# The first expert stage: 64 slots in fp32 for the seven experts with the fewest tokens, chosen on the chip

## The chip, the core and the metric

The kernel runs on one core of a Trainium2 chip. The metric is the device time of one launch in microseconds, the median of three runs. The engines in what follows are PE (TensorE, the matrix engine; PEld is its load of the stationary operand), DVE (VectorE), ACT (ScalarE), POOL (GpSimd) and SP (SyncE, which here issues the weight loads). Data comes from HBM over 16 DMA engines.

## What is computed

Two blocks in a row, on 256 tokens and 256 context tokens of width 1024. The first block has two layers; each ends in a routed mixture of 16 experts of which every token uses two. Layer 0 routes all 512 tokens, layer 1 only the 256 tokens. The second block has a third expert layer. The change is in layer 0's experts alone:

```python
def routed_moe(h2d, router_w, router_b, w_gate, w_up, w_down):
    ...                                   # every token: 2 experts of 16, weights wts
    counts = jnp.bincount(flat_e, length=N_EXPERTS)
    ...                                   # rows of the same expert brought together
    def expert_block(args):
        xblk, e = args
        hid = jax.nn.silu(xblk @ w_gate[e]) * (xblk @ w_up[e])
        return hid @ w_down[e]
```

Each weight matrix is 1024 by 1024 in fp32, 4 MiB, so an expert needs 12 MiB of weights. The 1024 assignments of a token to an expert are spread unevenly.

## The kernel before

The first expert stage is `moe0` (line 1172). `route_steps` ranks the experts for every token and gives each assignment a place among those of its expert; `counts` gives the number of assignments of each expert. From these a table `idx` of 16 columns is made: column x names the tokens of expert x, one in each of 128 slots. `gather(x)` (line 1219) brings these 128 rows from HBM by an indirect DMA on POOL's queue. `overflow` (line 1360) holds a loop for experts with more than 128 tokens. It stands in an `If` that every engine evaluates by loading one number from SBUF (lines 1370 and 1371); where no expert has more, all engines branch past it.

Then 16 experts follow, x = 0 to 15, in program order, each with three products: gate, up and down. They are staggered: up of x, gate of x + 1, down of x. A product (`product`, line 1556) has 8 steps `kt`. In each, the 128 by 1024 slice of the weight is split into `hi` (a copy to fp32r, on ACT, line 341) and `lo` (the rest, on DVE, line 329), and six matmuls of 512 columns add `xh·hi`, `xh·lo` and `xl·hi` for both column halves. The stationary operand is the tokens or the hidden values, transposed (`t8`, line 1540: eight transposes on PE, then `xh` on ACT and `xl` on DVE). Between the steps of a product stand, at step 2, `silu` and the product with `up`, and at step 5 the transposes that the next product needs. `store` writes the 128 rows of the expert to a DRAM tensor `yd`, from which at the end every token gathers its two rows.

Weights come through `wrows` (line 359): four tiles of 1 MiB for each matrix, from a ring of nine (`RING` is 7, and 2 more in this stage), issued by SP one after the other. SP waits for each ring place until the old tile is split. What stands in which order on an engine is decided by a scheduler when the program is built, by program order and the buffers that are free; each engine then works in that order. `u4`, a pool of 20 buffers of 128 by 1024, holds `hi`, `lo`, `xh`, `xl` and the rest; `u2` has three of 128 by 512.

The other two expert stages (`experts`, line 1717) already use column groups: with G = 2 in layer 1 there are 64 slots, and a step is two fp32 matmuls (line 1771), one for each column half of the unsplit weight, on columns 0 to 63 and 64 to 127 of PE.

Of the kernel before, what the change touches and what calls it, by code (L numbers as in the profile page):

```python
# [17 lines left out]
KT = 8  # L18
# [198 lines left out]
class K:  # L217
# [141 lines left out]
    def wrows(self, src, r0=0, n=1024, pairs=False):  # L359
# [8 lines left out]
        return Weights(tiles, 2)  # L368

# [740 lines left out]
    def route_steps(self, p, nb, l, after_counts=None):  # L1110
# [45 lines left out]
        e16 = self.C("e16").unsqueeze(1).to_broadcast([128, nb, 16])  # L1156
# [3 lines left out]
        def rest():  # L1160
            for k, oh in enumerate((oh1, oh2)):
                self.total(oh, e16, nb, out[:, k])
                self.total(oh, aff, nb, out[:, 4 + k])
# [6 lines left out]


    def moe0(self, X, htok, srow, kr, lg, modT):
# [42 lines left out]
        ti = self.sm(16)  # L1215
        self.copy(ti, pt[:, 0:16], "v")
        self.stt(idx, pt[:, 16:32], 128.0, ti, OP.mult, OP.add)

        def gather(x):
            xg = self.u4("xg")  # L1220
            nc.gpsimd.indirect_dma_start(
                out=xg, out_offset=None, in_=h2d[0:512],
                in_offset=bass.IndirectOffsetOnAxis(ap=idx[:, x:x + 1], axis=0))
            return xg

        xg = [gather(0), gather(1)]
        rest()
        ov = self.keep(8, "ov0").rearrange("p (k b) -> p k b", k=2)
        self.ts(ov, r, 127.5, op0=OP.is_gt)
        Wg, Wu, Wd = A["moe_w_gate"][0], A["moe_w_up"][0], A["moe_w_down"][0]  # L1230
        w = self.wrows(Wg[0], pairs=True)
# [8 lines left out]
        self.overflow(0, 512, 128, rt, cnt, ov, lambda: h2d, add)  # L1240


        last = 15 * 128
        pos = self.keep(8, "pos0").rearrange("p (k b) -> p k b", k=2)
        self.stt(pos, e, 128.0, r, OP.mult, OP.add)
# [13 lines left out]

        def silu(x, pg):  # L1260
            s[x] = self.u4("sg")
# [8 lines left out]
        def store(x, py):  # L1270
            y = self.u4("y") if x < 15 else held[2][:, 0]
            for half, p in enumerate(py):
                self.copy(y[:, half * 512:(half + 1) * 512], p, None if x == 15 else "s")
            if x < 15:
                nc.gpsimd.dma_start(yd[x * 128:(x + 1) * 128, :], y)
# [28 lines left out]
        for x in range(16):  # L1304
# [5 lines left out]
            def next_x(x=x):  # L1310
                if x < 15:
                    nxt["x"] = self.t8(xg[1])
# [3 lines left out]
            pu = self.product(xT, self.wrows(Wu[x], pairs=True) if x < 15 else wu, {2: flush, 5: next_x})  # L1316

            def hidden(x=x):
                nxt["h"] = self.t8(s.pop(x))

            if x < 15:
                xT = nxt["x"]
                pg = self.product(xT, self.wrows(Wg[x + 1], pairs=True), {2: lambda: times(x, pu), 5: hidden})
# [3 lines left out]
            if x < 15:  # L1327
                w = self.wrows(Wd[x], pairs=True)
            py = self.product(nxt["h"], w, {15: {2: collect}}.get(x, {}))
# [1364 lines left out]
```

## Time and profile before

| | |
|---|---|
| median of three runs | 2692.64 us (2692.07 to 2694.62) |
| profiled execution | 2689.91 us, of which the span from first to last instruction is 2688.1 us |
| busy in the span | PE 2324.9 us (86%), DVE 1401.4 us (52%), ACT 981.5 us (37%), POOL 61.3 us (2%) |
| HBM | 780.88 MB read, 295 GB/s over the span |
| first expert stage | about 485 to 1100 us |
| second expert stage | about 1329 to 1850 us |
| third expert stage | about 2230 to 2665 us |

Shares of the whole span mix stages with different limits. The rows below are taken from single stretches, whose limits in microseconds from the span's start each names. In a row of the view by stretch, "35.45 (x160)" is 35.45 us of busy time in 160 instructions. The DMA share is the mean busy share of the 16 DMA engines. A matmul in fp32 on a column group shows as two records.

### The profile page before, as it was taken

Reading aid. Unit: us, or ns where it says so; the run is one execution under the profiler, and the core shown is the slowest. Engines: PE = TensorE matmul, PEld = TensorE weight load, DVE = VectorE, ACT = ScalarE, POOL = GpSimd, SP = SyncE. Lnnn points to the kernel's source line nnn. Section 1 sums busy time; section 2 is a strip of 40 time slices with the busy share of each in tenths; the row PEclk is TensorE's granted clock in tenths of the full one; section 3 lists DMA queues with packets and bytes.
Section 4 is the critical chain, followed back from the end, with each engine's and each line's share of the span. In section 5 each row is a group of like instructions: output and inputs, shape, how many; then the busy total and the mean of one; then the engine's idle time right before and its main releaser. Section 6 shows DMA issues by size and latency. Waiting matters only on the chain.

```text
span 2688.1 us, 40516 instructions
## 1 busy us (share of the span) xinstructions
PE 2324.9 (86%) x16362; PEld 1589.2 (59%) x16363; DVE 1401.4 (52%) x2810; ACT 981.5 (37%) x1692; POOL 61.3 (2%) x57
## 2 busy tenths in 40 slices
PE   6999887799999999898898898997899977777765
PEld 4887666677777787675533443444888964323322
DVE  5675554888888888756314232324776751000001
ACT  3332332676767777446202221112545620000000
POOL 0000002000000001000000000000000000000000
PEclk8999999899999999999899999998899988777787
DMA  8157841799999998645499999987423449999997
GB/s 297 32 201 254 287 168 62 301 365 371 364 367 361 366 384 343 226 169 206 189 421 375 405 374 372 386 348 305 138 89 138 157 178 414 420 420 420 419 420 313
DMA packets 178600, 794.66 MB, mean 296 GB/s; under 512 B 18017, under 2 KB 33761, under 8 KB 104673
## 3 DMA queue, kind: packets, MB, share of 16 engines
q1 hardware_dynamic: 168048, 767.28, 73.3%
q0 software_dynamic: 5648, 20.45, 1.9%
q10 hardware_dynamic: 4704, 4.21, 0.5%
q8 instruction: 132, 2.16, 0.3%
q14 instruction: 68, 0.55, 0.1%
HBM read 780.88 MB, written 11.01 MB: 295 GB/s over the span
## 4 chain that ended last, share of the span: by engine, by line
PE 30%; DMA 20%; DVE 6%; ACT 1%; issue 1%; SPq 0%; DVEq 0%; ACTq 0%
PE ps L308 14%; PE ps L1771 7%; DMA w<-in_w_e_down_dram 6%; DMA w<-in_w_e_up_dram 5%; DMA w<-in_w_e_gate_dram 5%; PE ps L1785 4%; PE ps L1500 2%; PE ps L311 1%; DMA w<-in_moe_w_up_dram 1%; DMA w<-in_moe_w_down_dram 1%; DMA w<-in_w_in_dram 1%; PE ps L1713 1%; DVE sm L1664 1%; PE ps L1687 1%; DMA w<-in_moe_w_gate_dram 1%
## 5 line engine op out<-in xcount | busy, mean ns | idle before, releaser
L329 DVE TENSOR_TENSOR lo<-w,hi 128x1024 fp32r<-128x1024 f32 (+1 forms) x628 | 626.2, 1045 | 106.2 <-ACT hi L341 89.3
L341 ACT ACTIVATE hi<-w 128x1024 fp32r<-128x1024 f32 (+1 forms) x628 | 530.6, 913 | 95.6 <-PE ps L308 54.0
L1771 PE MATMUL ps<-w,xTs 128*32 128x256 f32 (+1 forms) x3072 | 405.9, 503 | 74.2 <-DMA w<-in_w_e_gate_dram 46.2
L1771 PEld LDWEIGHTS ps<-w,xTs 128*32 128x32 f32 (+1 forms) x3072 | 132.9, 128 | 291.2 <-issue 158.1
L1785 PE MATMUL ps<-w,hTs 128*32 128x256 f32 (+1 forms) x1536 | 217.2, 542 | 61.9 <-DMA w<-in_w_e_down_dram 53.6
L308 PE MATMUL ps<-lo,xh 128*128 128x512 f32 x768 | 243.0, 398 | 13.7 <-DVE lo L329 13.7
L308 PE MATMUL ps<-hi,xh 128*128 128x512 f32 x768 | 243.5, 398 | 7.5 <-ACT hi L341 7.5
L308 PE MATMUL ps<-hi,xl 128*128 128x512 f32 x768 | 238.0, 391 | 0.0
L1785 PEld LDWEIGHTS ps<-w,hTs 128*32 128x32 f32 (+1 forms) x1536 | 70.9, 136 | 191.0 <-issue 87.4
L308 PEld LDWEIGHTS ps<-lo,xh 128*128 128x128 f32 x768 | 141.1, 189 | 51.7 <-DVE lo L329 25.0
L308 PEld LDWEIGHTS ps<-hi,xh 128*128 128x128 f32 x768 | 140.6, 189 | 45.5 <-ACT hi L341 19.0
L308 PEld LDWEIGHTS ps<-hi,xl 128*128 128x128 f32 x768 | 144.6, 188 | 31.1
L329 DVE TENSOR_TENSOR sgs<-sgs,ps 128x512 f32<-128x512 f32 (+1 forms) x32 | 17.7, 553 | 266.2 <-PE ps L1771 266.2
L308 PE MATMUL ps<-hTh,hi 128*128 128x256 f32 x416 | 123.2, 296 | 0.8 <-ACT hi L341 0.8
L308 PE MATMUL ps<-hTh,lo 128*128 128x256 f32 x416 | 119.5, 287 | 2.0 <-DVE lo L329 2.0
L308 PE MATMUL ps<-hTl,hi 128*128 128x256 f32 x416 | 118.8, 286 | 0.0
L341 ACT ACTIVATE sgs<-ps 128x512 f32<-128x512 f32 (+1 forms) x32 | 15.7, 490 | 275.0 <-PE ps L1771 275.0
L308 PE MATMUL ps<-hh,hi 128*128 128x512 f32 (+1 forms) x272 | 106.1, 390 | 6.0 <-ACT hi L341 6.0
L308 PE MATMUL ps<-hl,hi 128*128 128x512 f32 (+1 forms) x272 | 101.1, 372 | 0.0
L308 PE MATMUL ps<-hh,lo 128*128 128x512 f32 (+1 forms) x272 | 101.0, 371 | 0.1
L320 ACT ACTIVATE hTs<-ps 128x512 f32<-128x512 f32 (+1 forms) x16 | 7.8, 490 | 234.9 <-PE ps L311 234.9
L341 ACT ACTIVATE xh<-ps 128x512 fp32r<-128x512 f32 x64 | 35.4, 595 | 135.8 <-PE ps L311 135.8
(567 smaller groups left out, 3650.7 us busy)
## 6 DMA issues: line engine op xcount, KB each, us to landing
w<-in_moe_w_gate_dram SPq DMA_DIRECT2D x128, 1024.0 KB, 7.7
w<-in_moe_w_up_dram SPq DMA_DIRECT2D x128, 1024.0 KB, 7.5
w<-in_moe_w_down_dram SPq DMA_DIRECT2D x128, 1024.0 KB, 9.0
w<-in_w_e_gate_dram SPq DMA_DIRECT2D x64, 1024.0 KB, 20.0
w<-in_w_e_down_dram SPq DMA_DIRECT2D x64, 1024.0 KB, 20.0
w<-in_w_e_up_dram SPq DMA_DIRECT2D x64, 1024.0 KB, 20.0
w<-in_ada_w_dram SPq DMA_DIRECT2D x48, 1024.0 KB, 7.1
w<-in_w_mod_dram SPq DMA_DIRECT2D x24, 1024.0 KB, 7.0
```

The source lines that it names most:

```text
L308: self.nc.tensor.matmul(out, lhsT, rhs, start=start, stop=stop)
L311: self.nc.tensor.transpose(out, in_, self.C("id"))
L320: self.nc.scalar.activation(out, in_, AF.Copy)
L329: self.nc.vector.tensor_tensor(out, a, b, op=op)
L341: self.nc.scalar.activation(out, in_, f, **kw)
L1500: self.nc.tensor.matmul(o, a[:, c].bitcast(FR), b, start=(k == 0 and j == 0 and m % 2 == 0), stop=(k == nk - 1 and j == 2), skip_group_che ...
L1664: nc.vector.tensor_reduce(mx, t, axis=AX.X, op=OP.max)
L1687: nc.tensor.matmul(po[j][0][r, c], v[n][:, g * 64:g * 64 + 64], at[i][:, n * 128:(n + 1) * 128], start=(n == 0), stop=(n == 3), tile_posit ...
L1713: self.nc.tensor.matmul(acc[b][dg], owT[r, b * 128:(b + 1) * 128], y[r, :n], start=(first and (b == 0 or G == 2)), stop=False, skip_group_ ...
L1771: self.nc.tensor.matmul(p[g * S:(g + 1) * S, :], a[:, s0:s0 + S], w(kt, g * n, (g + 1) * n), start=(kt == 0), stop=(kt == KT - 1), tile_po ...
L1785: self.nc.tensor.matmul(py[dg * S:(dg + 1) * S, :], hT[:, j * 128 + g * S:j * 128 + (g + 1) * S], w(ft, dg * n, (dg + 1) * n), start=(ft = ...
```

## The change

The experts are ranked on the chip by their number of assignments (`ranked`, DVE). Expert 0 is put first whatever its load, since its gate weights are loaded before the ranking is known. The next eight by load take the places 2, 4, ... 14 and 15, the seven smallest the places 1, 3, ... 13. A place of the first kind has 128 slots as before. One of the second kind, "few", has 64. Its tokens and hidden values are transposed but not split; its weights aren't split either; a step is two fp32 matmuls of 512 columns on 64 columns of PE each (`product` inside `moe0`). Its result lies with one column half on partitions 0 to 63 and the other on 64 to 127, and is stored by two DMAs. Which expert stands at a place is read by SP from SBUF into a register, and the weight loads take their address from it (`chosen`). The table `idx` is put into the new order, and positions and the test for the overflow loop go by the capacity of each expert.

```diff
+    def chosen(self, e, *W):
+
+        i = self.nc.values_load(e, engines=[mybir.EngineType.SP], min_val=0, max_val=15)
+        return [w[bass.ds(i, 1)].rearrange("a d f -> (a d) f") for w in W]
+
...
 
-        def rest():
+        def rest(more=()):
             for k, oh in enumerate((oh1, oh2)):
-                self.total(oh, e16, nb, out[:, k])
+                for row, o in more or ((self.C("e16"), out),):
+                    self.total(oh, row.unsqueeze(1).to_broadcast([128, nb, 16]), nb, o[:, k])
                 self.total(oh, aff, nb, out[:, 4 + k])
...
+    def ranked(self, cnt):
+        nc = self.nc
+        key, rank, place, base, cap, t = (self.sm(16) for _ in range(6))
+        e16 = self.C("e16")
+        self.stt(key, cnt, 16.0, e16, OP.mult, OP.add)
+        self.ts(key[:, 0:1], key[:, 0:1], 65536.0, op0=OP.add)
+        rows = lambda v: v.unsqueeze(1).to_broadcast([128, 16, 16])
+        cols = lambda v: v.unsqueeze(2).to_broadcast([128, 16, 16])
+        sel, w = (self.u2("place")[:, :256].rearrange("p (i e) -> p i e", i=16) for _ in range(2))
+        self.tt(w, rows(key), cols(key), OP.is_gt)
+        nc.vector.tensor_reduce(rank, w, axis=AX.X, op=OP.add)
+        self.ts(t, rank, 7.5, op0=OP.is_gt)
+        self.ts(place, rank, 8.0, 16.0, OP.is_equal, OP.mult)
+        self.stt(place, t, -17.0, place, OP.mult, OP.add)
+        self.stt(place, rank, 2.0, place, OP.mult, OP.add)
+        self.ts(base, place, 96.0)
+        self.stt(base, t, 32.0, base, OP.mult, OP.add)
+        self.ts(cap, rank, 8.5, -64.0, OP.is_gt, OP.mult)
+        self.ts(cap, cap, 128.0, op0=OP.add)
+        self.tt(sel, rows(place), cols(e16), OP.is_equal)
+        self.mul(w, sel, rows(e16))
+        expert = self.sm(16, I32, name="order")
+        self.reduce_int(expert, w)
+        return base, cap, sel, w, expert
+    def reduce_int(self, out, v):
+        t = self.sm(16)
+        self.nc.vector.tensor_reduce(t, v, axis=AX.X, op=OP.add)
+        self.copy(out, t, "v")
 
...
         idx = self.keep(16, "idx", I32)
-        ti = self.sm(16)
+        ti, tj, idx0 = self.sm(16), self.sm(16), self.sm(1, I32)
         self.copy(ti, pt[:, 0:16], "v")
-        self.stt(idx, pt[:, 16:32], 128.0, ti, OP.mult, OP.add)
+        self.stt(idx0, pt[:, 16:17], 128.0, ti[:, 0:1], OP.mult, OP.add)
+        self.stt(tj, pt[:, 16:32], 128.0, ti, OP.mult, OP.add)
+
+        few = lambda x: x % 2 == 1 and x < 15
+        slots = lambda x: slice(96 * x + 32 * (x % 2), 96 * x + 32 * (x % 2) + (64 if few(x) else 128))
 
         def gather(x):
-            xg = self.u4("xg")
+            xg, n = self.u4("xg"), 64 if few(x) else 128
+            at = (idx[:, x:x + 1] if x else idx0)[0:n]
             nc.gpsimd.indirect_dma_start(
-                out=xg, out_offset=None, in_=h2d[0:512],
-                in_offset=bass.IndirectOffsetOnAxis(ap=idx[:, x:x + 1], axis=0))
+                out=xg[0:n], out_offset=None, in_=h2d[0:512],
+                in_offset=bass.IndirectOffsetOnAxis(ap=at, axis=0))
             return xg
 
-        xg = [gather(0), gather(1)]
-        rest()
-        ov = self.keep(8, "ov0").rearrange("p (k b) -> p k b", k=2)
-        self.ts(ov, r, 127.5, op0=OP.is_gt)
-        Wg, Wu, Wd = A["moe_w_gate"][0], A["moe_w_up"][0], A["moe_w_down"][0]
-        w = self.wrows(Wg[0], pairs=True)
+        xg = [gather(0)]
+        base, cap, sel, tmp, order = self.ranked(cnt)
+        self.mul(tmp, sel, tj.unsqueeze(1).to_broadcast([128, 16, 16]))
+        self.reduce_int(idx, tmp)
+        xg.append(gather(1))
+        pos, capt = (self.keep(8, n).rearrange("p (k b) -> p k b", k=2) for n in ("pos0", "ov0"))
+        rest(((base, pos), (cap, capt)))
+
+        over = self.sm(8).rearrange("p (k b) -> p k b", k=2)
+        self.tt(over, r, capt, OP.subtract)
+        ov = capt
+        self.ts(ov, over, -0.5, op0=OP.is_gt)
+        self.tt(cap, cnt, cap, OP.subtract)
+        self.ts(cap, cap, 0.0, op0=OP.max)
+        self.add(pos, pos, r)
+        W = A["moe_w_gate"][0], A["moe_w_up"][0], A["moe_w_down"][0]
+        Wg, Wu, Wd = [u[0] for u in W]
+        w = self.wrows(Wg, pairs=True)
         ready = [self.wparts(w, kt) for kt in range(READY)]
 
...
-        self.overflow(0, 512, 128, rt, cnt, ov, lambda: h2d, add)
-        last = 15 * 128
-        pos = self.keep(8, "pos0").rearrange("p (k b) -> p k b", k=2)
-        self.stt(pos, e, 128.0, r, OP.mult, OP.add)
+        def all_tokens():
+            for k, oh in enumerate(self.oh):
+                self.total(oh, self.C("e16").unsqueeze(1).to_broadcast([128, 4, 16]), 4, e[:, k])
+            self.copy(r, over, "v")
+            return h2d
+        self.overflow(0, 512, 0, rt, cap, ov, all_tokens, add)
+        last = slots(15).start
         self.stt(pos, ov, 4096.0, pos, OP.mult, OP.add)
...
+        def product(x, a, w, inside={}):
+            if not few(x):
+                return self.product(a, w, inside)
+            p = self.ps()
+            for kt in range(KT):
+                if kt in inside:
+                    inside[kt]()
+                for g in range(2):
+                    nc.tensor.matmul(p[64 * g:64 * g + 64], a(kt), w(kt, 512 * g, 512 * g + 512), start=kt == 0,
+                                     stop=kt == KT - 1, tile_position=(0, 64 * g))
+            return [p]
+        def tokens_of(x, xg):
+            if not few(x):
+                return self.t8(xg)
+            p, t = self.ps(), self.u2("xf")
+            for k in range(KT):
+                nc.tensor.transpose(p[:, 64 * k:64 * k + 64], self.pair_block(xg[0:64], k), self.C("id")[0:64, 0:64])
+            self.copy(t, p)
+            return lambda kt: t[:, 64 * kt:64 * kt + 64]
+        def hidden_of(x, s):
+            if not few(x):
+                return self.t8(s)
+            p, t = self.ps(), self.u2("hf")
+            for j in range(4):
+                self.tr(p[:, 128 * j:128 * j + 128], self.pair_block(s, j))
+            self.copy(t, p)
+            return lambda ft: t[:, 128 * (ft % 4) + 64 * (ft // 4):128 * (ft % 4) + 64 * (ft // 4) + 64]
...
         def store(x, py):
+            if few(x):
+                y = self.u2("yf")
+                self.copy(y, py[0], "s")
+                for g in range(2):
+                    nc.gpsimd.dma_start(yd[slots(x)][:, 512 * g:512 * g + 512], y[64 * g:64 * g + 64])
+                return
...
             def next_x(x=x):
                 if x < 15:
-                    nxt["x"] = self.t8(xg[1])
+                    nxt["x"] = tokens_of(x + 1, xg[1])
                     if x < 14:
                         xg[1] = gather(x + 2)
 
-            pu = self.product(xT, self.wrows(Wu[x], pairs=True) if x < 15 else wu, {2: flush, 5: next_x})
+            pu = product(x, xT, self.wrows(Wu, pairs=True) if x < 15 else wu, {2: flush, 5: next_x})
 
             def hidden(x=x):
-                nxt["h"] = self.t8(s.pop(x))
+                nxt["h"] = hidden_of(x, s.pop(x))
 
             if x < 15:
                 xT = nxt["x"]
-                pg = self.product(xT, self.wrows(Wg[x + 1], pairs=True), {2: lambda: times(x, pu), 5: hidden})
+                down = Wd
+                Wg, Wu, Wd = self.chosen(order[0:1, x + 1:x + 2], *W)
+                pg = product(x + 1, xT, self.wrows(Wg, pairs=True), {2: lambda: times(x, pu), 5: hidden})
             else:
                 times(x, pu)
                 hidden()
             if x < 15:
-                w = self.wrows(Wd[x], pairs=True)
-            py = self.product(nxt["h"], w, {15: {2: collect}}.get(x, {}))
+                w = self.wrows(down, pairs=True)
+            py = product(x, nxt["h"], w, {15: {2: collect}}.get(x, {}))
             if x == 14:
-                wu, w = self.wrows(Wu[15], pairs=True), self.wrows(Wd[15], pairs=True)
+                wu, w = self.wrows(Wu, pairs=True), self.wrows(Wd, pairs=True)
                 weights()
```

DVE's queue between the routing and the `If`. Before, from the eight comparisons that build the token table to the load of the number on which the `If` is decided (`rt` holds ranks and weights of each token, `ov` the overflow test, `mi` the number):

```order
L324 TENSOR_SCALAR hits<-ciota,rt_4419 128x128 x8
L329 TENSOR_TENSOR sm<-sm,con 128x64
L329 TENSOR_TENSOR sm<-sm,aff_4351 128x64
L318 COPY sm<-ps 128x16
L1090 TENSOR_REDUCE rt_4419<-sm 128x4
L338 SCALAR_TENSOR_TENSOR idx<-ps,sm 128x16
```

Now, from the same eight comparisons (`place` is a 16 by 16 table on every partition, `order` the experts by place):

```order
L324 TENSOR_SCALAR hits<-ciota,rt_4419 128x128 x8
L318 COPY sm<-ps 128x16
L338 SCALAR_TENSOR_TENSOR sm<-ps,sm 128x1
L338 SCALAR_TENSOR_TENSOR sm<-ps,sm 128x16
L338 SCALAR_TENSOR_TENSOR sm<-cnt_4413,con 128x16
L324 TENSOR_SCALAR sm<-sm 128x1
L329 TENSOR_TENSOR place<-sm 128x256
L1191 TENSOR_REDUCE sm<-place 128x16
```

Before, the number for the `If` (`mi`) is 13 rows behind the comparisons, with the three `lo` splits of the first product behind it. Now it is 45 rows behind them, the last of them the end of this piece, with the three splits ahead of it:

```order
L329 TENSOR_TENSOR sm<-rt_4419,ov_4491 128x8
L324 TENSOR_SCALAR sm<-sm 128x16
L1171 RECIPROCAL sm<-sm 128x4
L324 TENSOR_SCALAR ov_4491<-sm 128x8
L329 TENSOR_TENSOR lo<-w,hi 128x1024
L329 TENSOR_TENSOR rt_4419<-rt_4419,sm 128x8
L329 TENSOR_TENSOR lo<-w,hi 128x1024 x2
L318 CAST ci_4540<-sm 128x16
L1470 TENSOR_REDUCE mi_4542<-sm 128x1
```

PE's queue around the up product of an expert. Before, at step 5 of it (`xg` the gathered tokens of the next expert):

```order
L308 MATMUL ps<-lo,xh 128x512 x2
L308 MATMUL ps<-hi,xl 128x512 x2
L311 MATMUL ps<-con,xg 128x128 x8
L308 MATMUL ps<-hi,xh 128x512 x2
L308 MATMUL ps<-lo,xh 128x512 x2
```

Now the same product of a few expert, with the row ahead of it and the three behind it (`xf` its tokens, `sf` its hidden values):

```order
L308 MATMUL ps<-hi,xl 128x512 x2
L1330 MATMUL ps<-w,xf 64x512 x4
L311 MATMUL ps<-con,xg 128x128
L1330 MATMUL ps<-w,xf 64x512 x4
L311 MATMUL ps<-con,xg 128x128 x7
L1330 MATMUL ps<-w,xf 64x512 x8
L308 MATMUL ps<-hi,xh 128x512 x2
L311 MATMUL ps<-con,sf 128x128 x4
L308 MATMUL ps<-lo,xh 128x512 x2
```

So 16 matmuls stand where 48 stood, in three pieces with transposes between them, and the transposes of `sf` come behind the first two matmuls of the next product. The gate product is cut in the same way, the down product stands in one piece. On DVE the elementwise product that makes `sf` stands ahead of the splits of that next product.

SP's queue ahead of the `If`. Before:

```order
L366 DMA w<-in_moe_w_up_dram 128x2048 x3
L366 DMA w<-in_moe_w_gate_dram 128x2048 x3
L1370 TENSOR_LOAD mi_4497
L1370 ISA x2
L1371 COMPARE_AND_BRANCH
```

Now, up to the first of 13 pairs of rows that load an entry of `order` into a register; the load of `mi` follows them, and the two other entries are loaded later:

```order
L2724 DMA x<-in_xtok_dram 128x1024
L366 DMA w<-in_moe_w_up_dram 128x2048 x3
L366 DMA w<-in_moe_w_gate_dram 128x2048 x2
L372 TENSOR_LOAD order
L372 ISA x2
```

Ahead of the `If` eight weight tiles (gate and up of expert 0) are issued now, where it was nine before: the first tile of the next gate matrix has moved behind the branch. Behind it each tile loaded by register has one register instruction ahead of its DMA.

## Rows read from the trace of the kernel before

**Rows 1.** One tile, `yd`; duration ns min/median/max, first and last start us
```profile
L1275 POOL DMA_DIRECT2D yd<-y x15: 563/570/593, 537.6 to 1055.8; - x15
```

**Rows 2.** Busy time by stretch, three stages; last three columns clock, DMA share, GB/s
```profile
core 0: us, PE busy (x) PEld busy (x) DVE busy (x) ACT busy (x) POOL busy (x), PEclk, DMA share, GB/s
...
612.00:649.00 37.00, 35.45 (x160) 28.33 (x159) 31.29 (x30) 26.58 (x33) 2.44 (x2) 1.00 0.94 363
...
1455.00:1490.00 35.00, 32.20 (x147) 10.71 (x147) 9.93 (x24) 1.82 (x3) 0.00 (x0) 1.00 1.01 422
...
2250.00:2300.00 50.00, 35.35 (x364) 15.28 (x357) 3.27 (x10) 2.47 (x6) 0.00 (x0) 0.76 1.01 420
```

**Rows 3.** Who waited for whom, 540 to 1056: total us, times, longest
```profile
PEld ps L308 <- DVE lo L329: 23.1, 24, 1.0
PEld ps L308 <- ACT hi L341: 16.4, 24, 0.7
```

**Rows 4.** The same for SP's queue
```profile
SPq L366 <- DVE lo L329: 441.0, 165, 6.0
```

**Rows 5.** DMA, 540 to 1056: packets, MB, share; KB each, us to landing
```profile
DMA packets 27921, 189.29 MB, mean 367 GB/s; under 512 B 3105, under 2 KB 3105, under 8 KB 6561
...
q1 hardware_dynamic: 24000, 174.72, 87.7%
q0 software_dynamic: 3888, 14.16, 6.7%
...
xg<-h2d,idx POOLq DMA_INDIRECT x13, 10.9
```

**Rows 6.** Timeline of PE in the second expert stage: start us, us, work
```profile
1359.66 7.04 PE L1771 MATMUL ps<-w,xTs 128*64 128x512 f32 x32
...
1374.77 0.75 PE L311 MATMUL ps<-con,sgs 128*128 128x128 f32 x4
```

**Rows 7.** Timeline of PE in the first expert stage
```profile
617.77 1.11 PE L311 MATMUL ps<-con,xg 128*128 128x128 f32 x8
```

**Rows 8.** Groups by line, 540 to 1056: busy us, mean ns, idle before
```profile
L329 DVE TENSOR_TENSOR lo<-w,hi 128x1024 fp32r<-128x1024 f32 x335 | 385.7, 1219 | 26.7 <-ACT hi L341 23.3
```

**Rows 9.** Timeline at the start of the first expert stage
```profile
472.35 0.42 DVE L1135 TENSOR_REDUCE sm<-cmp 128x64 f32<-128x256 f32 x1
...
473.52 0.17 DVE L329 TENSOR_TENSOR sm<-sm 128x16 f32<-128x16 f32 x1
473.73 0.17 DVE L329 TENSOR_TENSOR sm<-sm,con 128x16 f32<-128x16 f32 x1
...
478.05 0.18 DVE L318 COPY sm<-ps 128x16 f32<-128x16 f32 x1
...
478.61 0.22 DVE L329 TENSOR_TENSOR sm<-sm,aff 128x64 f32<-128x64 f32 x1
478.75 0.34 DVE L1090 TENSOR_REDUCE rt<-sm 128x4 f32<-128x64 f32 x2
...
479.22 0.16 DVE L1369 TENSOR_REDUCE mi<-cnt 128x1 int32<-128x16 f32 x1
...
481.62 3.48 DVE L329 TENSOR_TENSOR lo<-w,hi 128x1024 fp32r<-128x1024 f32 x3
...
485.22 1.99 PE L311 MATMUL ps<-con,xg 128*128 128x128 f32 x8 [7.20 <-DVEq L1371]
```

**Rows 10.** Line 1370: duration ns min/median/max, first and last start
```profile
L1370 SPq TENSOR_LOAD <-mi x2: 289/373/457, 479.4 to 1316.3; - x2
...
L1370 PEldq TENSOR_LOAD <-mi x2: 313/400/487, 479.4 to 1852.6; - x2
...
L1370 SPq FUSED_REGOPS  x2: 164/168/173, 479.9 to 1316.6; - x2
```

**Rows 11.** Line 1371, the same columns
```profile
L1371 PEldq COMPARE_BRANCH  x2: 3499/3500/3501, 480.0 to 1853.1; - x2
```

**Rows 12.** Timeline of SP's queue, third expert stage
```profile
2249.70 0.33 SPq L366 DMA_DIRECT2D w<-in_w_e_up_dram  x1
```

More of the change, by code (lines that the diff above doesn't have):

```diff
@@ L1155, in route_steps @@
         out = self.keep(6 * nb, f"rt{l}").rearrange("p (j b) -> p j b", j=6)
-        e16 = self.C("e16").unsqueeze(1).to_broadcast([128, nb, 16])
         for k, oh in enumerate((oh1, oh2)):
             self.total(oh, pre, nb, out[:, 2 + k])
-        def rest():
+        def rest(more=()):
             for k, oh in enumerate((oh1, oh2)):
-                self.total(oh, e16, nb, out[:, k])
+                for row, o in more or ((self.C("e16"), out),):
+                    self.total(oh, row.unsqueeze(1).to_broadcast([128, nb, 16]), nb, o[:, k])
                 self.total(oh, aff, nb, out[:, 4 + k])
@@ L1258, in moe0 @@
         s, pg = {}, self.product(xT, w, ready=ready)
+        def product(x, a, w, inside={}):
[25 more added lines that the diff above has]
+            return lambda ft: t[:, 128 * (ft % 4) + 64 * (ft // 4):128 * (ft % 4) + 64 * (ft // 4) + 64]
         def silu(x, pg):
-            s[x] = self.u4("sg")
+            s[x] = self.u2("sf") if few(x) else self.u4("sg")
             for half, p in enumerate(pg):
@@ L1274, in store @@
             if x < 15:
-                nc.gpsimd.dma_start(yd[x * 128:(x + 1) * 128, :], y)
+                nc.gpsimd.dma_start(yd[slots(x)], y)
             return y
@@ L1384, in overflow @@
             self.ts(pad, self.C("lane")[:, 0:1], float(T), op0=OP.add)
-            pi = self.keep(n, f"pi{l}", I32)
+            pi = self.u4("pi").bitcast(I32)[:, 0:n]
             self.copy(pi, pad.to_broadcast([128, n]), "v")
```

## The prediction

> **What bounds the kernel now.** I read the stores of the first expert stage first, since they are its clock. Fifteen stores of `yd` start between 537.6 and 1055.8 us [rows 1], so an expert takes 518.2 / 14 = 37.0 us. Then the view by stretch [rows 2]: in 37 us PE is busy for 35.45 at a granted clock of 1.00, the upper of its two levels (2.4 GHz), DVE for 31.29, ACT for 26.58. PE sets the pace. What is left of its time ended with the splits: 24 waits each for `lo` (23.1 us) and `hi` (16.4 us) [rows 3], two per expert in the stretch. SP, in turn, waited 441.0 us for ring places [rows 4]: the loads follow PE. But they are not far behind. All 16 DMA engines were busy 94% of the time [rows 2], at 367 GB/s on average [rows 5]. So the question is how much of a shorter PE time the loads can follow.
>
> **What the change removes.** Seven experts at odd places need 16 unsplit matmuls for a product instead of 48 and a split. The same product, 64 slots and two column groups, stands in the second expert stage: 32 records in 7.04 us [rows 6]. I take that duration, since shape, column groups and clock are the same. Three products: 21.1 us. Twelve transposes (eight of tokens, four of hidden values), at 1.11 / 8 = 0.14 us [rows 7]: 1.7 us. Behind a column-group product four transposes took 0.75 us where 4 x 0.14 = 0.56 would do [rows 6, 7], so a change between the two kinds costs about 0.19 us. The order of PE shows 14 such changes for each few expert: four inside the gate and four inside the up product, and six at the ends of the three products. 14 x 0.19 = 2.7 us. A few expert is then 21.1 + 1.7 + 2.7 = 25.5 us, and a pair of one full and one few expert 37.0 + 25.5 = 62.5 us, against 74.0.
>
> The last row shows this cost; the Trainium skill, "TensorEngine Tiling (Array Packing)", Key Properties, says that a change of tiling mode drains TensorE. It gives no price; if the drain were free the pair would be 59.8 us, by the row it is 62.5.
>
> Waits that move: a full product behind a few one finds its splits done early in one case of three (up behind down), which saves about 23.1 / 24 = 1.0 us [rows 3]. In another (gate behind up), DVE's order puts the elementwise product for `sf` ahead of the splits, so the first `lo` (1.22 us [rows 8]) starts late, some 1 us lost. I set these against each other at nothing; with neither hidden the pair is 64.5. ACT and DVE lose three products' splits per pair and cannot become the bound.
>
> **What the loads can follow.** A pair needs 24 tiles of 1 MiB, 25.17 MB. Gather and store move 128 rows of 4 KiB each way for a full expert and 64 for a few one: 1.05 + 0.52 = 1.57 MB. Together 26.74 MB. The rate when the queue is always full: 422 GB/s in the second stage and 420 in the third, with the DMA share at 1.01 [rows 2]. At 420 a pair takes 63.7 us. The other end is the pace of this stage itself, with stores and gathers mixed in: 87.7 + 6.7 = 94.4% busy for 367 GB/s [rows 5], so 389 GB/s when fully busy, 68.7 us a pair. I take 420, since the queue will be full as in those stages. The loads also have a lead: the ring holds nine tiles, 9.44 MB, 22.5 us at 420. Needed is 7 x (63.7 - 62.5) = 8 us. So PE still sets the pace in the forecast, with the lead used up by a third. A gather lands 10.9 us after its issue [rows 5] and is issued an expert ahead; even twice that is hidden. In stretches where PE waits for loads its clock could fall: it was 0.76 with PE busy for 35.35 of 50 us, but 1.00 with 32.20 of 35 [rows 2]; here it would be about 62.5 of 63.7.
>
> Stage: 7 x (74.0 - 62.5) = 80 us less.
>
> **What it adds, on the path.** All engines load `mi` and branch. Before, `mi` was written at 479.22; the rest of the time to 485.22, when PE starts, was three `lo` splits (3.48 us, to 485.10) for which PE waits behind the branch [rows 9]. PE's own load and branch (0.49 and 3.50 us [rows 10, 11]) lay beside them. Now `mi` is 45 rows behind the comparisons, with the splits ahead of it. From 478.05 there are some 37 small DVE instructions, 0.13 us apart if they are independent, 0.21 if chained [rows 9]: 4.8 to 7.8 us. Then seven on 256 elements at about 0.45 (a sum over 256 took 0.42 [rows 9]), 3.2 us, and the splits, 3.5 us. So `mi` is written at 489.5 to 492.5, and what it hid comes behind it: 0.49 + 3.50 + 0.1. PE starts at 493.6 to 496.6, 8.4 to 11.4 us later. I take 10.
>
> SP loads 13 entries of `order` ahead of its branch, 0.37 + 0.17 us each [rows 10], 7 us, beside DVE's work. Behind each waits the rest of SP's queue, that is the gate tiles of place 1. They are first needed two full products after PE's start, 24 us later, and take 10 us. Hidden; if not, a few us once. Issue by register adds perhaps 0.17 us [rows 10] to 0.33 [rows 12] for each tile, and SP has 62.5 / 24 = 2.6 us for one.
>
> Sum: 80 - 10 = 70 us less. Own time of the profiled execution 2689.9 (2688.1 of span and 1.8 around it) gives 2620; the median lies 2.7 us above it, so 2692.6 - 70 = **2623**. Bounds of this case: with no price for the changes between kinds, the loads set the end at 420 GB/s: 518 - (7 x 63.7 - 22.5) = 95, less 8.4, so 2606. With 64.5 a pair and 11.4 at the start: 66 - 11, 2637.
>
> **Rivals.**
> 1. *The loads stay at the stage's own 389 GB/s.* For: stores and gathers stay. Against: that rate comes from a queue that was often half empty. 7 x 68.7 - 22.5 = 458, 60 less, minus 10: **2643**.
> 2. *367 GB/s is already all there is beside the compute of this stage.* For: the share of 0.94. Against: 420 elsewhere, in stages that also compute. A pair is 72.9; 7 x 72.9 - 22.5 = 488, 30 less, minus 10: **2673**. The Trainium skill, "DMA: Bandwidth & Descriptors", Specifications, gives an HBM limit of about 358 GB/s per core. By it a pair would be 74.7 and the time 2685; the 420 of this trace disagrees, and the measurement decides.
> 3. *Slower: loads by register take long at SP.* No row shows such an issue, only the static one (0.33 us [rows 12]) and register work (0.17 [rows 10]). Every tile of places 1 to 15 is issued so, 168 of them in the seven pairs. If one took more than (518 - 10) / 168 = 3.0 us on SP, all gain would be gone; at 3.2 the seven pairs take 538, 20 more, plus 10: **2723**. It decides only at six times what the rows add up to.
> 4. *The change doesn't do what it says*: one of the seven smallest has over 64 tokens, and the loop of `overflow` runs. The reference on its inputs (seed 0) gives loads of 27 to 105; with expert 0 (59) set first, the seven smallest are 61, 57, 56, 48, 47, 42 and 27. So it shouldn't; where it did, every such expert reads 12.6 MB again, 30 us at 420 GB/s, for two of them **2683** or more.
>
> **How the numbers follow.** Forecast 0.58, rival 1 0.25, rival 2 0.08, rival 3 0.05, rival 4 0.01, and 0.03 for small gains from causes I don't see. A measurement tells about 0.2% from no change, that is 2687 to 2698. Faster: 0.58 + 0.25 + 0.07 of rival 2, 0.01 and some of the rest, 0.92; within 0.2%: 0.03; slower: 0.05. The range runs from the lower bound of the forecast with a little room, 2602, past rival 1 to 2656 (rival 1 with 2 us more a pair); outside lie rival 2 to 4 and a few per cent below.
>
> **What would show it.** Stores in the changed stage come in pairs 62 to 64 us apart; few products take 7.0 us; PE's start in this stage is at 494 to 497; the DMA rate between the stores is 410 to 425 GB/s with a share near 1.00. If PE waits for `w` of few products from the second pair on at under 400 GB/s, rival 1 holds; if SP's issues are long with DMA engines idle, rival 3. The forecast is wrong if a pair takes over 66 us, or if few products take well over 7.1 us.

## The result, and the profile of the changed kernel

The changed kernel takes 2645.5 us (median of 4 runs, 2640.36 to 2651.04), the kernel before 2692.36 beside it (4 runs): 0.9826 of the time, interval 0.9803 to 0.985. It is 47 us faster; forecast were 70. The time lies in the range, and near that of rival 1 (2643), whose mechanism turns out not to be the cause.

The profiled execution took 2643.11 us (span 2641.5), 46.8 less than that of before. Three stretches share this, by two stores of `yd` and PE's start:

| stretch | before | after | difference |
|---|---|---|---|
| first instruction to PE's start in the stage | 485.22 | 496.11 | +10.9 |
| PE's start to the last store in [rows 1], that of place 14 | 570.6 | 516.0 | -54.6 |
| from there to the end | 1632.3 | 1629.4 | -2.9 |

The forecast had +10 and -80 for the first two rows. So the missing 23 us are to be looked for between PE's start and the last store.

The stores of the full experts' results are now a pair apart. The timeline of POOL after the change, answering to [rows 1] (start us, us, work, idle before and what ended it):

```profile
543.18 0.60 POOL L1374 DMA_DIRECT2D yd<-y  x1 [33.53 <-ACT y L320]
605.51 0.59 POOL L1374 DMA_DIRECT2D yd<-y  x1 [32.85 <-ACT y L320]
673.65 0.59 POOL L1374 DMA_DIRECT2D yd<-y  x1 [37.14 <-ACT y L320]
...
946.37 0.59 POOL L1374 DMA_DIRECT2D yd<-y  x1 [37.20 <-ACT y L320]
1012.11 0.58 POOL L1374 DMA_DIRECT2D yd<-y  x1 [36.41 <-ACT y L320]
```

The first pair takes 62.3 us, next to the forecast's 62.5. Then five take 68.2 each, and the last 65.7. What the later pairs have that the first has not is seen in the busy time by stretch, answering to [rows 2]: the first pair, the second, a later one, and four short stretches inside the later one.

```profile
core 0: us, PE busy (x) PEld busy (x) DVE busy (x) ACT busy (x) POOL busy (x), PEclk, DMA share, GB/s
543.20:605.50 62.30, 60.08 (x270) 36.57 (x268) 32.94 (x32) 28.85 (x35) 3.92 (x5) 1.00 1.01 411
605.50:673.65 68.15, 63.77 (x270) 38.83 (x268) 32.76 (x32) 28.73 (x35) 4.03 (x5) 0.95 1.01 415
...
741.80:810.00 68.20, 63.82 (x270) 38.83 (x268) 32.76 (x32) 28.75 (x35) 4.05 (x6) 0.95 0.99 391
769.00:771.00 2.00, 0.36 (x3) 0.26 (x2) 0.28 (x1) 1.85 (x3) 0.96 (x2) 1.00 1.00 418
773.00:775.00 2.00, 2.00 (x7) 1.56 (x6) 0.90 (x2) 2.00 (x4) 0.00 (x0) 0.51 1.02 410
...
793.00:795.00 2.00, 0.49 (x4) 0.00 (x0) 0.00 (x0) 1.42 (x2) 0.00 (x0) 1.00 0.95 336
797.00:799.00 2.00, 2.00 (x6) 1.55 (x5) 2.00 (x3) 2.00 (x4) 0.00 (x0) 0.50 0.95 401
```

With the same number of instructions (270), PE is busy for 3.7 us more in the later pair than in the first, and idle for 2.2 us more. Twice in the pair it stands still for most of two microseconds (0.36 and 0.49 busy), and a little later its granted clock is at half, the lower of its two levels. What it waits for at these places is in ACT's timeline of the same pair:

```profile
769.15 0.60 ACT L320 ACTIVATE yf<-ps 128x512 f32<-128x512 f32 x1 [15.23 <-PE ps L1330]
769.64 2.00 ACT L341 ACTIVATE hi<-w 128x1024 fp32r<-128x1024 f32 x2
...
793.59 0.60 ACT L341 ACTIVATE sf<-ps 128x512 f32<-128x512 f32 x1 [3.04 <-PE ps L1330]
794.08 7.68 ACT L341 ACTIVATE hi<-w 128x1024 fp32r<-128x1024 f32 x8
```

and in PE's:

```profile
751.21 0.73 PE L308 MATMUL ps<-lo,xh 128*128 128x512 f32 x2 [0.39 <-DVE lo L329]
...
770.74 0.73 PE L308 MATMUL ps<-hi,xh 128*128 128x512 f32 x2 [1.64 <-ACT hi L341]
...
773.09 1.05 PE L308 MATMUL ps<-hi,xl 128*128 128x512 f32 x2
...
795.18 0.73 PE L308 MATMUL ps<-hi,xh 128*128 128x512 f32 x2 [1.69 <-ACT hi L341]
796.44 0.82 PE L308 MATMUL ps<-lo,xh 128*128 128x512 f32 x2 [0.53 <-DVE lo L329]
```

`yf` is the copy of a few expert's result out of PSUM, `sf` its silu. Both can only run when PE has finished that expert's product. Each stands in ACT's queue ahead of the `hi` splits for the product that comes next on PE. ACT sat idle for 15.23 us ahead of `yf`. So the next full product starts with no split ready: PE waits 1.64 and 1.69 us, and some 2 us later two matmuls take 1.05 us, where they take about 0.62 at a clock of 1.00. In the first pair ACT's order had two splits ahead of `yf`, and only the `sf` place stalled PE (1.69 us again); its clock stayed at 1.00. That ACT works its queue in order is also what the Trainium skill says ("PSUM — Partial Sum Buffer", Engine vs sequencer instructions: strict FIFO); the trace agrees, the splits having started 0.49 us behind `yf` and `sf`.

The loads weren't what PE waited for. The waits of SP in 605 to 878 us (total us, times, longest), answering to [rows 4], are for ring places, none for the DMA queues:

```profile
SPq L366 <- DVE lo L329: 109.2, 48, 3.7
SPq L366 <- PE ps L1330: 107.4, 48, 5.8
```

In the DMA view of the same stretch (KB each, median us to landing) a tile lands 8 to 11 us after its issue:

```profile
w<-in_moe_w_down_dram SPq DMA_DIRECT2D x32, 1024.0 KB, 10.8
w<-in_moe_w_up_dram SPq DMA_DIRECT2D x32, 1024.0 KB, 10.0
w<-in_moe_w_gate_dram SPq DMA_DIRECT2D x32, 1024.0 KB, 8.1
```

Yet the DMA share is 0.99 in the later pair, at 391 GB/s. It doesn't say that the engines gave all they can: the second pair of the same run had 415 GB/s at a share of 1.01, and took the same 68.15 us. Nor does 391 GB/s say what sets the pace. A pair needs 26.74 MB, and 26.74 MB in 68.2 us are 392 GB/s: once every load waits for a ring place, the rate follows from the length of the pair, whatever that length comes from.

The start of the stage, answering to [rows 9] (DVE, then PE):

```profile
478.93 1.65 DVE L324 TENSOR_SCALAR hits<-ciota,rt 128x128 bf16<-128x128 f32 x8
...
487.48 1.22 DVE L329 TENSOR_TENSOR lo<-w,hi 128x1024 fp32r<-128x1024 f32 x1
488.69 2.35 DVE L329 TENSOR_TENSOR lo<-w,hi 128x1024 fp32r<-128x1024 f32 x2
491.04 0.16 DVE L1470 TENSOR_REDUCE mi<-sm 128x1 int32<-128x16 f32 x1
```

```profile
496.11 1.95 PE L311 MATMUL ps<-con,xg 128*128 128x128 f32 x8 [15.26 <-PEq L1472]
```

`mi` is written at 491.04 and PE begins 5.1 us later. `hits`, the eight comparisons that no part of the change touches, was at 476.10 before and is at 478.93 here, 2.8 us that come from ahead of the stage. From `hits` to PE's start it is 17.18 us against 9.12: 8.1 us belong to the change.

### The profile page after: what moved, and what is told of

The parts are those of the page before. It is cut to its first block, busy times and chain, and to the rows that moved or that the text cites. A ratio compares the mean times of both kernels' runs of the same rounds, so it can differ in the third digit from the quotient of the medians.

```text
span 2641.5 us, 39523 instructions
## 1 busy us (share of the span) xinstructions
PE 2259.2 (86%) x15998; PEld 1450.4 (55%) x15999; DVE 1197.1 (45%) x2641; ACT 805.7 (31%) x1489; POOL 55.9 (2%) x64
## 3 DMA queue, kind: packets, MB, share of 16 engines
HBM read 779.04 MB, written 9.18 MB: 298 GB/s over the span
## 5 line engine op out<-in xcount | busy, mean ns | idle before, releaser
L329 DVE TENSOR_TENSOR lo<-w,hi 128x1024 fp32r<-128x1024 f32 (+1 forms) x460 | 434.3, 983 | 189.1 <-ACT hi L341 174.8
L341 ACT ACTIVATE hi<-w 128x1024 fp32r<-128x1024 f32 (+1 forms) x460 | 370.4, 863 | 102.4 <-PE ps L308 54.5
L308 PE MATMUL ps<-hi,xh 128*128 128x512 f32 x432 | 141.4, 410 | 21.0 <-ACT hi L341 21.0
L308 PE MATMUL ps<-lo,xh 128*128 128x512 f32 x432 | 142.8, 413 | 5.6 <-DVE lo L329 5.5
L308 PE MATMUL ps<-hi,xl 128*128 128x512 f32 x432 | 141.0, 409 | 0.0
L308 PEld LDWEIGHTS ps<-hi,xh 128*128 128x128 f32 x432 | 83.5, 198 | 56.7 <-ACT hi L341 38.3
L1330 PE MATMUL ps<-w,xf 128*64 128x512 f32 x448 | 105.0, 601 | 0.0
L308 PEld LDWEIGHTS ps<-lo,xh 128*128 128x128 f32 x432 | 81.6, 195 | 28.7 <-DVE lo L329 11.8
L308 PEld LDWEIGHTS ps<-hi,xl 128*128 128x128 f32 x432 | 85.7, 198 | 19.0
L308 PEld LDWEIGHTS ps<-hTh,hi 128*128 128x128 f32 x416 | 80.7, 194 | 3.3 <-issue 1.3
```

Of the source, the lines that this page charges most:

```text
L308: self.nc.tensor.matmul(out, lhsT, rhs, start=start, stop=stop)
L329: self.nc.vector.tensor_tensor(out, a, b, op=op)
L341: self.nc.scalar.activation(out, in_, f, **kw)
L1330: nc.tensor.matmul(p[64 * g:64 * g + 64], a(kt), w(kt, 512 * g, 512 * g + 512), start=kt == 0, stop=kt == KT - 1, tile_position=(0, 64 * g))
```

## Experiments

Two theories for the 68.2 us of a pair. *Order*: ACT's queue keeps the splits behind `yf` and `sf`, PE stalls, and its clock falls. *Loads* (rival 1): the loads don't follow at more than about 390 GB/s, and PE's stalls only fit themselves into that. Every time below stands beside runs of the kernel before on the same chip (2690.19 us, 9 runs, for the first four kernels, 2689.25, 9 runs, for the last three).

### The copy `yf` behind the splits

```diff
-                self.copy(y, py[0], "s")
+                self.tc.keep_in_program_order(nc.scalar.activation(y, py[0], AF.Copy))
```

The program is the same; on ACT, `yf` now stands behind the splits that come before it in program order.

> Only the copy of a few expert's result out of PSUM (yf, on ACT) is pinned behind the splits that are written ahead of it in the program; before, it stood ahead of all eight splits of the next up product in ACT's queue. Theory (order): in the changed kernel ACT waits 15 us in front of that copy with split work behind it, PE then starts the up product cold, sits idle 1.6 us, and for some 4 us after that gets half its clock; the same happens a second time per pair, behind the silu of sf. Taking away one of the two should bring a pair from 68.2 to about 65.2 us, the whole from 2645 to about 2628. Rival (loads): the stage can't draw more than about 400 GB/s with its stores and gathers, so the pair stays at 68.2 us and the time at 2645.

Measured: 2623.28 us (2621.58 to 2624.99, 2 runs), ratio 0.9753, interval 0.9733 to 0.9772. Pairs take 62.9 to 64.5 us. One stretch of it by busy time:

```profile
735.00:800.00 65.00, 62.26 (x281) 37.19 (x278) 32.84 (x32) 28.96 (x35) 5.54 (x7) 1.00 1.01 415
```

From PE's start to the last store it takes 496.4 us (494.55 to 990.96), where the changed kernel took 516.0. The order theory holds: one moved instruction per pair brings 19.6 us, somewhat more than expected (pairs of 62.9 to 64.5 us against 65.2), and the same loads run at 415 GB/s. The stretch shown lies mostly in the one of the first six pairs in which the clock stayed at 1.00 behind the gap at `sf`; in the five others it is 0.97.

### `yf` and the silu `sf`

```diff
-                self.act(s[x][:, half * 512:(half + 1) * 512], p, AF.Silu)
+                i = nc.scalar.activation(s[x][:, half * 512:(half + 1) * 512], p, AF.Silu)
+                if few(x):
+                    self.tc.keep_in_program_order(i)
...
-                self.copy(y, py[0], "s")
+                self.tc.keep_in_program_order(nc.scalar.activation(y, py[0], AF.Copy))
```

> Both are pinned: the copy of yf behind the first three splits of the up product, the silu of sf behind all eight splits of the down product. Theory (order): both stalls and both stretches at half clock go, a pair falls from 68.2 to 62.3 (what the first pair of the changed kernel took) or to 63.7 us where the loads then set the end at 420 GB/s; six pairs by 4.5 to 5.9 us, so 2610 to 2618. Rival (loads at about 400 GB/s): 68.2 a pair and 2645 as before the edit.

Measured: 2622.3 us (2621.91 to 2623.74, 4 runs), ratio 0.975, interval 0.9734 to 0.9766: no different from the one before, and short of the 2610 to 2618 that were expected. The first pairs are short (59.4 and 60.6), then they are 64.6 to 65.2, the last 67.3. The first and a late pair by busy time, and the waits of ACT in 605 to 878 us:

```profile
541.98:601.38 59.40, 59.40 (x270) 36.69 (x268) 32.94 (x32) 28.84 (x35) 3.86 (x5) 1.00 1.01 412
727.80:793.00 65.20, 61.11 (x270) 36.36 (x268) 33.34 (x32) 29.55 (x35) 4.02 (x6) 1.00 1.01 413
```

```profile
ACT hi L341 <- DMA w<-in_moe_w_up_dram: 44.4, 8, 10.9
...
ACT hi L341 <- DMA w<-in_moe_w_gate_dram: 23.4, 16, 3.0
...
ACT hi L341 <- DMA w<-in_moe_w_down_dram: 14.9, 16, 2.8
```

Now the splits wait for the weights themselves, 83 us in about four pairs; after the change no such wait stood in this view of the same stretch. In the first pair, which the ring's lead carries, PE was busy all the time. In the late one it is idle for 4.1 us, behind splits that wait for the loads, at 413 GB/s.

### Half the weights for the few experts

On top of the last one, each few expert loads two of the four tiles of every matrix and uses each twice. It leaves out half of these experts' weights.

```diff
+            if twice and j % 2:
+                tiles.append(tiles[-1])
+                continue
...
```

> The pinned kernel, with each few expert loading only two of the four tiles of each weight matrix and using them twice: it leaves out half of the few experts' weights, so 20.4 MB instead of 26.7 MB a pair. Theory (the pinned kernel's 65 us a pair are the loads, 26.7 MB at 412 GB/s): the pairs fall to PE's own time, 59 to 61 us as in the first two pairs, which the lead of the ring carries; the stage is some 5 x 4.5 = 22 us shorter, 2600. Rival (PE's or ACT's waits set the 65 us): pairs stay near 65, 2622.

Measured: 2593.74 us (2592.69 to 2594.78, 2 runs), ratio 0.9646, interval 0.9628 to 0.9663. Every pair but the last takes 58.8 us:

```profile
716.98:775.78 58.80, 58.80 (x270) 36.74 (x268) 32.76 (x32) 28.73 (x35) 3.95 (x6) 1.00 0.89 348
```

PE is never idle. So 58.8 us is PE's own time for a pair, and the 65 us of the pinned kernel are the loads; the builder's order, which differs a little between the two kernels, isn't the reason, since the pinned kernel's own first pair took 59.4. The same trace prices the work of a few expert (PE's timeline):

```profile
730.99 0.63 PE L311 MATMUL ps<-con,sf 128*128 128x128 f32 x4
731.38 0.71 PE L308 MATMUL ps<-hi,xh 128*128 128x512 f32 x2
...
735.64 7.09 PE L1333 MATMUL ps<-w,hf 128*64 128x512 f32 x32
742.66 0.73 PE L308 MATMUL ps<-hi,xh 128*128 128x512 f32 x2
...
749.68 1.17 PE L1343 MATMUL ps<-con,xg 64*128 64x64 f32 x8
750.79 0.73 PE L308 MATMUL ps<-hi,xh 128*128 128x512 f32 x2
...
755.09 4.51 PE L1333 MATMUL ps<-w,xf 128*64 128x512 f32 x20
759.53 1.22 PE L311 MATMUL ps<-con,sg 128*128 128x128 f32 x8
760.69 2.79 PE L1333 MATMUL ps<-w,xf 128*64 128x512 f32 x12
763.41 0.73 PE L308 MATMUL ps<-hi,xh 128*128 128x512 f32 x2
```

Read from start to start, a few product without anything inside takes 7.02 us (735.64 to 742.66). One with eight transposes inside takes 8.32 (755.09 to 763.41). What the eight take without a change of kind is in the trace of before, where they stand between the matmuls of a full product:

```profile
617.77 1.11 PE L311 MATMUL ps<-con,xg 128*128 128x128 f32 x8
618.64 0.70 PE L308 MATMUL ps<-hi,xh 128*128 128x512 f32 x2
```

From start to start they take 0.87, though their row says 1.11 [rows 7]. That leaves 8.32 - 7.02 - 0.87 = 0.43 us for the two changes of kind around them, about 0.2 each, as the forecast took. A few expert's own transposes take 1.11 (its tokens, 749.68 to 750.79) and 0.39 (its hidden values, 730.99 to 731.38, though that row says 0.63). With two products cut by transposes and one whole, a few expert is 2 x 7.45 + 7.02 + 1.11 + 0.39 = 23.4 us. The 0.75 of [rows 6] was a row with nothing behind it: its length holds the end of the last instruction, and isn't a price from start to start.

### PE's gap filled

In each of the two gaps of a pair PE runs one more matmul, whose result nobody uses: ahead of an up product behind a few down, and ahead of a down product behind a few gate (`fill` marks both). It takes PE 1.1 us, where 1.4 was expected. ACT's order stays that of the changed kernel.

```diff
+                if w.fill:
+                    self.tc.keep_in_program_order(nc.tensor.matmul(self.ps(), self.C("id"), X[0][:, 0:512], start=True,
+                                                                   stop=True))
...
```

> The order of the changed kernel is kept; at the start of the full products that stall (up behind a few down, down behind a few gate) PE gets one fp32 matmul of 128 by 512 that nothing uses, some 1.4 us of work, to fill the gap. It tells the clock from the wait. If the half clock comes from PE's idle gap, it stays at 1.00 and a pair falls by the 3.7 us that its busy time grew over the first pair's, to about 64.5, the whole to about 2623. If the clock falls for another reason, or the loads set the pace, a pair stays at 68.2 or gets 1 to 2 us longer, 2645 to 2655.

Measured: 2634.0 us (2632.97 to 2635.04, 2 runs), ratio 0.9793, interval 0.9773 to 0.9812. The steady pairs take 65.8 us, and the clock is at 1.00 all through:

```profile
740.00:806.00 66.00, 63.47 (x275) 37.15 (x274) 32.80 (x33) 28.97 (x37) 4.02 (x5) 1.00 1.02 409
```

So the half clock came from PE's standing still: more work on PE and nothing moved on ACT, and a pair is 2.4 us shorter. Expected were 64.5 us a pair and 2623; where the other 1.3 us went isn't shown. The loads' 65 us lie close to 65.8, so how much more the clock would give back with faster loads stays open. The totals (2634.0 against 2645.5) are no measure of it, since PE began the stage at 490.70 here, with `hits` 5 us earlier; the pairs are.

### The ranking alone

All 16 experts keep 128 slots and the split; the ranking, the order table and the weight loads by register stay.

```diff
-        self.stt(base, t, 32.0, base, OP.mult, OP.add)
+        self.stt(base, place, 32.0, base, OP.mult, OP.add)
-        self.ts(cap, rank, 8.5, -64.0, OP.is_gt, OP.mult)
+        self.ts(cap, rank, 99.5, -64.0, OP.is_gt, OP.mult)
...
-        few = lambda x: x % 2 == 1 and x < 15
-        slots = lambda x: slice(96 * x + 32 * (x % 2), 96 * x + 32 * (x % 2) + (64 if few(x) else 128))
+        few = lambda x: False
+        slots = lambda x: slice(128 * x, 128 * x + 128)
```

> All 16 places get 128 slots and the split product as in the kernel before; the ranking on the chip, the new order and the loads by register stay. So it has the cost of the change without its gain. Theory: only the later start of the stage is paid, some 8 us (PE starts at about 496 against 485, of which 2.8 us came from ahead of the stage), 37.0 us an expert: 2692 + 8 = 2700. Rival (loads by register are slow): an expert takes longer than 37.0 us and the time lies above 2710.

Measured: 2698.34 us (2693.44 to 2702.44, 6 runs), ratio 1.0029, interval 1.0015 to 1.0042: 8 us slower. Its first and last stores of this kind lie at 546.44 and 1063.82, 517.4 us for 14 experts against 518.2 [rows 1]. An expert is as long as before; the loads by register cost nothing that shows, and rival 3 is out. What remains is the start, 16.71 us from `hits` to PE instead of 9.12, and these 7.6 us make up nearly all of the 8.

### The number for the branch ahead of the splits

```diff
-        ready = [self.wparts(w, kt) for kt in range(READY)]
+        ready = []
...
-        self.overflow(0, 512, 0, rt, cap, ov, all_tokens, add)
+        self.overflow(0, 512, 0, rt, cap, ov, all_tokens, add,
+                      lambda: ready.extend(self.wparts(w, kt, True) for kt in range(READY)))
...
```

The three splits now stand behind the instruction that makes the number.

> The three lo splits that DVE makes ahead of the number that decides the branch (487.5 to 491.0 us after the change) are put behind it; nothing else is moved. Theory (they are a cost of the change's own, since PE's branch, 3.5 us, can only begin once the number is there): PE begins the stage some 3.5 us earlier, near 492.5 by the trace after, less if the splits now end last; the time 2645 - 3.5 = 2641 to 2642. Rival (PE would wait for the splits instead, which it needs at once): no change, 2645.

Measured: 2637.77 us (2633.58 to 2643.44, 4 runs), ratio 0.9804, interval 0.9789 to 0.9819. This overlaps the interval of the changed kernel, so the total alone doesn't decide. The trace does (DVE, then PE):

```profile
475.08 1.65 DVE L324 TENSOR_SCALAR hits<-ciota,rt 128x128 bf16<-128x128 f32 x8
...
483.80 0.16 DVE L1471 TENSOR_REDUCE mi<-sm 128x1 int32<-128x16 f32 x1
483.88 3.48 DVE L1658 TENSOR_TENSOR lo<-w,hi 128x1024 fp32r<-128x1024 f32 x3
```

```profile
488.75 1.95 PE L311 MATMUL ps<-con,xg 128*128 128x128 f32 x8 [11.75 <-PEq L1474]
```

From `hits` to PE's start it is 13.67 us where it was 17.18: 3.5 us, as expected. In the five other traces with the splits ahead of the number it is 16.7 to 16.9, so 3.0 us may be nearer. The splits lie beside the branch again, as they did before the change. The steady pairs are unchanged (68.15 us).

### Both together

`yf` and `sf` behind the splits, and the number for the branch ahead of the first three.

> Both the order of ACT's instructions (yf and silu behind the splits traced ahead of them) and the place of the three lo splits. Theory of the order, with the loads as the limit of what is left: the stage's pairs stay at 65 us, bound by the loads, so an earlier start of PE brings only what the loads allow, between nothing and 3.5 us: 2619 to 2622. Rival (PE is the limit of the pinned kernel): the whole 3.5 us, 2619 or less, with pairs under 65.

Measured: 2618.74 us (2614.76 to 2623.15, 5 runs), ratio 0.9733, interval 0.972 to 0.9746. It beats the kernel before by 70 us and the changed kernel by some 25 (0.9826 against 0.9733 of 2690). From `hits` to PE's start it takes 13.89 us. The pairs from the third on are 64.3 to 65.4 us again (67.0 the last):

```profile
857.25:922.37 65.12, 61.15 (x270) 36.39 (x268) 33.39 (x32) 29.56 (x35) 4.03 (x5) 1.00 1.01 414
```

Its tiles land 19 to 22 us after their issue (605 to 878 us), twice as late as after the change. At 24 tiles in 65 us that is seven or eight tiles issued and not yet landed, against three or four after the change (8 to 11 us, 24 tiles in 68.2):

```profile
w<-in_moe_w_up_dram SPq DMA_DIRECT2D x36, 1024.0 KB, 18.8
w<-in_moe_w_down_dram SPq DMA_DIRECT2D x34, 1024.0 KB, 20.3
w<-in_moe_w_gate_dram SPq DMA_DIRECT2D x33, 1024.0 KB, 21.6
```

Whether the earlier start adds anything to the order's gain can't be told from the totals: 0.9733 and 0.975 have intervals that overlap. For the same reason this run doesn't decide between its two expectations; that the loads are the limit rests on the run with half the weights.

## Why the prediction was right, and where it wasn't

**The sign and the range** held: the few experts' products are short and the loads can follow most of the way. The mechanism of the forecast held only in part. Its worst end was 64.5 us a pair and 2637 us, and its own sign of being wrong, a pair of over 66 us, came: five pairs took 68.2. The time lies in the range only because the range was drawn past rival 1, whose mechanism is refuted below; that part is luck.

**The step that failed** is the one on the waits. The prediction set a wait saved against a wait lost and took nothing, with 64.5 us a pair as its worst end. Of the three places where a full product stands behind a few one, it counted on 1.0 us saved at the first (up behind down) and 1 us lost at the second (gate behind up), and said nothing of the third (down behind gate). It looked at DVE's order there and not at ACT's. The first is the place of `yf`, where PE waits 1.64 us; at the second PE waits 0.39 (at 751.21 us); the third is the place of `sf`'s silu, where it waits 1.69 and 0.53. Each of `yf` and `sf` costs PE a stall at a product's begin, a product that runs on with splits just made, and, from the second pair on, half the clock for some 4 us. From PE's start to the last store the changed kernel needs 516.0 us, the kernel with `yf` and `sf` behind the splits 495.0 (493.96 to 988.93). The order's price is thus 21 us of the 25 that are missing in this stretch. A small misreading beside it: [rows 3] has 24 waits of each kind in some 14 experts, which is fewer than the two per expert that the prediction names; the sum doesn't use it.

**The pace of PE** was mis-sized in the other direction: 62.5 us forecast, 58.8 measured with half the few experts' loads. A few expert takes about 23.4 us there from start to start, not 25.5. The price of a change of kind was right (about 0.2 us against 0.19), by luck, since it was the difference of two row lengths that each hold the end of a last instruction. The number was too high: in that order each gate and up product is interrupted once and not twice, so four changes stand inside products, and the six at the ends of products add nothing to the start-to-start times of the few ones. Together that is 0.9 us instead of 2.7. The full expert is then 35.4, not 37.0, since with the splits ready it loses its waits [rows 3]; PE was busy for 35.45 us of an expert before [rows 2]. In the changed kernel's own order, with each gate and up product interrupted twice, no pair shows PE's time undisturbed. The first pair's 62.3 us, so close to the forecast, was a sum of two errors: less work on PE (60.1 busy), and 2.2 us of stall (1.69 and 0.53) for splits behind `sf`. The Trainium skill, "Perfetto Trace Analysis", Per-engine timelines, says that the end of a TensorE instruction in a profile is computed and not observed; the trace agrees: the rows of 1.11 and 0.63 us are 0.87 and 0.39 from start to start.

**What the loads can follow**: forecast 63.7 us at 420 GB/s, measured 65 at 413 to 415. So the loads, and not PE, are the bound of the kernel with ACT's order put right; 1.3 us a pair. The 389 GB/s of rival 1 was the rate of a queue that waits for ring places, in this kernel as in the one before; that its 2643 us came so near the result is chance. The prediction's own test ("PE waits for `w` of few products") spoke against it, the second pair's 415 GB/s too, and pairs of 62.9 to 64.5 us at 415 GB/s with nothing but `yf` moved refute it. Rival 2 with its 367 GB/s falls by the same rows. The page cited there gives 358; the Trainium skill has a second figure, about 435 GB/s for one core alone over its 16 DMA engines ("Perfetto Trace Analysis", Roofline), and the 413 to 415 measured here are nearer to that one.

Rival 4 didn't come about: with the change 779.04 MB are read from HBM instead of 780.88, 1.8 MB less for the seven times 64 rows that aren't gathered, so no expert was read again.

**The start**: +10 forecast, within 8.4 to 11.4. Measured are 8.1 of the change's own by `hits`; that the whole came to +10.9 is chance, with 2.8 from elsewhere. Two terms were off: `mi` is written 12.1 us behind `hits`, where 13.4 to 16.4 were forecast, and PE begins 5.1 us behind `mi`, where 4.1 were. And 3.0 to 3.5 of the 8.1 are the splits ahead of `mi`, as the prediction worked out.

**Places of the few products**: 21 of them are in the stretch, as taken, but one lies ahead of the first store (gate of place 1) and the last pair has two. Read by pairs alone, the gain is 518.2 - 468.9 = 49.3; the first store adds 5.3. The sum is not touched by it.

**What stays open**: why `hits` lies between 473.9 and 481.6 us in nine traces of the same work ahead of the stage, and why the builder's order has two splits ahead of `yf` in the first pair and none later.

## What to carry to other kernels

Where a change makes some products short, read the order on every engine that both drains a product and prepares the next: a drain ahead of the preparation is a stall of the matrix engine, however idle the other engine is on average. Price a change between kinds of instructions from start to start with something behind it, never from the length of a last row. And a DMA share near 1 doesn't prove that the loads are the limit: ask who waits (the issuer for a place, or the consumer for the data) and how long after its issue a transfer lands.

## What the runs showed of the hardware

After PE had stood still for 1.64 or 1.69 us inside dense work, its granted clock fell to 0.50, some 1 to 3 us later and for three to four us. That followed ten of the twelve such gaps of the changed kernel's stage (592 to 976 us) and five of the six with `yf` moved; behind the others, the first one of the changed kernel among them, it stayed at 1.00. One unused matmul in each gap kept it there. The falls cost about as much as the gaps: 3.7 us more busy time in a pair with two falls, where the two gaps are 3.3 us.

A change between fp32 matmuls on 64 columns and transposes on 128 took about 0.2 us from start to start (8.32 us with eight transposes inside a product, 7.02 without, 0.87 for the eight alone).
